# Loading three rows of the fourth tile early, on the second DMA queue, in a layer-norm kernel

## The chip, the cores and the metric

The kernel runs on one core of a Trainium2 chip. The metric is device time in microseconds (us) for one execution. Before the change it is 318.01 us, the median of three runs (317.99 to 318.68).

## The reference

The input `x` is 32 x 512 rows of 1024 floats, 64 MiB (67.11 MB) in all, and every row is normalized by its own mean and variance:

```
mean = np.mean(x, axis=-1, keepdims=True)
var = np.var(x, axis=-1, keepdims=True)
return ((x - mean) / np.sqrt(var + eps)).astype(np.float32)
```

There is no scale and no shift, so nothing but `x` is read, and 67.11 MB are written.

## The kernel before, in words

The 16384 rows are 128 blocks of 128 rows. The kernel calls one block's share of a partition a row, so that a "row" below is 128 partitions x 1024 floats, 512 KiB. Line 11 cuts the 128 rows into 15 tiles of 2 to 10 rows:

```
TILES = (4, 6, 10, 10, 10, 10, 10, 10, 10, 10, 10, 10, 10, 6, 2)
```

In memory, partition p holds K consecutive rows of a tile (`"(p k) d -> p k d"`), so a tile of K rows is, for each partition, one contiguous piece of K x 4 KiB on both sides.

All tiles live in one ring buffer in on-chip memory with room for 50 rows (`RING`). The plan gives each tile its place, starting over at 0 when the tile would not fit. The first six tiles (4 + 6 + 4 x 10 = 50 rows) fill the ring once; the seventh tile lies on the places of the first two, the eighth on those of the third, and so on. Tiles are counted from zero below where they carry a letter: L0 to L14 are the loads and S0 to S14 the stores of tiles 0 to 14. The fourth tile is tile 3.

For each tile, in program order:

- L122: one load of the tile, issued from SyncE (SP), into its place in the ring.
- L68: VectorE (DVE) takes two statistics instructions per row, each over 512 floats.
- L57 to L92: GpSimd (POOL) combines them into minus the mean and the sum of squares, for the whole group of rows at once.
- L95: ScalarE (ACT) takes the square root; L99: DVE the reciprocal; L101: POOL the product of minus the mean and the reciprocal.
- L103: ACT normalizes each row in place, in the ring.
- L127: one store of the tile, issued from ACT's own queue.

A group is a whole tile, except for the last three tiles, where it is at most 6 rows. The order of instructions on each engine is the program's order; it is written out by hand and not planned.

Loads therefore all go through SP's DMA queue (q1 in the profile) and stores all through ACT's (q10). Each load or store counts up one of eight completion semaphores, which the framework gives out in turn. Two kinds of waits come of that. A load into a place that was used before waits until the store of that place has landed: L6 waits for S0 and S1, L7 for S2, L8 for S3. And a transfer that gets a semaphore that an earlier one used waits until that one has landed: in the program before, L5 waits in this way for L0.

Of the kernel before, what the change touches and what calls it, by code (L numbers as in the profile page):

```python
# [1 line left out]

# [4 lines left out]


TILES = (4, 6, 10, 10, 10, 10, 10, 10, 10, 10, 10, 10, 10, 6, 2)  # L10

RING = 50


GROUP = 10
FINE = 6
LAST = 3


@with_exitstack  # L20
def kernel(
    ctx: ExitStack,
    tc: tile.TileContext,
    x: bass.AP,
    eps: bass.AP,
    out: bass.AP,
):
    nc = tc.nc
    P = nc.NUM_PARTITIONS
    eps_val = float(eps) if not isinstance(eps, bass.AP) else 1e-5  # L30

    x2 = x.flatten_outer_dims()
    o2 = out.flatten_outer_dims()
    N, D = x2.shape
    BN_MAX = nc.vector.BN_STATS_FMAX
    NSUB = D // BN_MAX
    H = 2 * NSUB
    assert sum(TILES) * P == N

    rings = ctx.enter_context(tc.tile_pool(name="rings", bufs=1))  # L40
    st = ctx.enter_context(tc.tile_pool(name="st", bufs=3))
    sm = ctx.enter_context(tc.tile_pool(name="sm", bufs=10))

    fdt = mybir.dt.float32
    AF = mybir.ActivationFunctionType
    ALU = mybir.AluOpType

    ring = rings.tile([P, RING, D], fdt)
    eps_t = rings.tile([P, 1], fdt)

    def rows_of(a, row, K):
        return a[row * P : (row + K) * P].rearrange("(p k) d -> p k d", p=P)

    def pool_sum(o, terms):
        G = terms.shape[1]
        half = sm.tile([P, GROUP, 2], fdt, name="half")
        nc.gpsimd.tensor_tensor(  # L57
            out=half[:, :G], in0=terms[:, :, 0:2], in1=terms[:, :, 2:4], op=ALU.add
        )
        nc.gpsimd.tensor_tensor(  # L60
            out=o, in0=half[:, :G, 0], in1=half[:, :G, 1], op=ALU.add
        )

    def group(xs, G):
        stats = st.tile([P, GROUP, NSUB, 6], fdt, name="stats")
        for k in range(G):
            for s in range(NSUB):
                nc.vector.bn_stats(  # L68
                    out=stats[:, k, s, :],
                    in_=xs[:, k, s * BN_MAX : (s + 1) * BN_MAX],  # L70
                )

        parts = stats[:, :G].rearrange("p g s (h c) -> p g (s h) c", h=2)
        mean4, m2 = parts[:, :, :, 1], parts[:, :, :, 2]
        nmean = sm.tile([P, GROUP], fdt, name="nmean")
        dev = sm.tile([P, GROUP, H], fdt, name="dev")
        ss = sm.tile([P, GROUP], fdt, name="ss")
        pool_sum(nmean[:, :G], mean4)
        nc.gpsimd.tensor_scalar(  # L79
            out=nmean[:, :G], in0=nmean[:, :G], scalar1=-1.0 / H, scalar2=None, op0=ALU.mult  # L80
        )
        nc.gpsimd.tensor_tensor(  # L82
            out=dev[:, :G],
            in0=mean4,
            in1=nmean[:, :G].unsqueeze(2).to_broadcast([P, G, H]),
            op=ALU.add,
        )
        nc.gpsimd.tensor_mul(out=dev[:, :G], in0=dev[:, :G], in1=dev[:, :G])  # L88
        nc.gpsimd.tensor_scalar(  # L89
            out=dev[:, :G], in0=dev[:, :G], scalar1=float(D // H), scalar2=None, op0=ALU.mult  # L90
        )
        nc.gpsimd.tensor_tensor(out=dev[:, :G], in0=dev[:, :G], in1=m2, op=ALU.add)  # L92
        pool_sum(ss[:, :G], dev[:, :G])
        std = sm.tile([P, GROUP], fdt, name="std")
        nc.scalar.activation(  # L95
            out=std[:, :G], in_=ss[:, :G], func=AF.Sqrt, bias=eps_t, scale=1.0 / D
        )
        rstd = sm.tile([P, GROUP], fdt, name="rstd")
        nc.vector.reciprocal(out=rstd[:, :G], in_=std[:, :G])  # L99
        nmr = sm.tile([P, GROUP], fdt, name="nmr")  # L100
        nc.gpsimd.tensor_mul(out=nmr[:, :G], in0=nmean[:, :G], in1=rstd[:, :G])  # L101
        for k in range(G):
            nc.scalar.activation(  # L103
                out=xs[:, k, :],
                in_=xs[:, k, :],
                func=AF.Identity,
                bias=nmr[:, k : k + 1],
                scale=rstd[:, k : k + 1],
            )

    plan, row, pos = [], 0, 0
    for K in TILES:
        if pos + K > RING:
            pos = 0
        plan.append((K, row, pos))
        row += K
        pos += K

    with tc.manual_schedule():
        nc.vector.memset(eps_t, eps_val)  # L120
        for t, (K, row, pos) in enumerate(plan):
            nc.sync.dma_start(out=ring[:, pos : pos + K, :], in_=rows_of(x2, row, K))  # L122
            step = FINE if t >= len(TILES) - LAST else GROUP
            for g in range(0, K, step):
                G = min(step, K - g)
                group(ring[:, pos + g : pos + g + G, :], G)
            nc.scalar.dma_start(out=rows_of(o2, row, K), in_=ring[:, pos : pos + K, :])  # L127


# [1 line left out]
_INS = ['x', 'eps']  # L131
_OUTS = [((32, 512, 1024), 'float32')]

_NUMBERS = {'eps': 1e-05}


# [26 lines left out]
```

## Time and profile before

| | |
|---|---|
| median of 3 runs | 318.01 us |
| the profiled execution's own time | 318.5 us |
| its span in the profile | 316.6 us |
| DVE busy | 156.5 us, 49% |
| ACT busy | 152.6 us, 48% |
| POOL busy | 37.5 us, 12% |
| moved by DMA | 134.25 MB, mean 424 GB/s over the span |
| loads, queue q1 | 2160 packets, 67.11 MB, 49.6% of 16 engines' span |
| stores, queue q10 | 2160 packets, 67.11 MB, 49.1% |

The span is the part of the execution that the profile shows, from the first instruction of the program to the last; the other 1.9 us of the profiled execution lie around it. The two queues' shares say how much of the time of the 16 DMA engines went into packets of loads and of stores. Busy shares of DVE, ACT and POOL are for the whole span. A DMA issue shows up twice: as a short instruction on the issuing engine's queue (SPq, ACTq), and as packets on the 16 DMA engines. A load or store has 9 packets on each of these: one for each of the 8 partitions that the engine serves, and one of 4 bytes that counts the semaphore up (2160 = 15 x 16 x 9).

### The profile page before, as it was taken

How to read it: one execution, taken by the hardware profiler on the slowest of the kernel's cores; microseconds unless marked ns; L12 is line 12 of the kernel's file. 1: busy time of each engine (PE TensorE's matmuls, PEld its weight loads, DVE VectorE, ACT ScalarE, POOL GpSimd, SP SyncE). 2: the span in 40 equal slices, each digit the busy share in tenths (PEclk: the TensorE clock that was granted, in tenths of full speed). 3: DMA queues.
4: the chain of work that ended last, by engine and by line, in shares of the span. 5: the costliest groups of instructions: out<-in, count | busy, mean ns of one | idle time of the engine just before them, and what ended most of it. 6: DMA issues, size and time to landing. Idle time of an engine off the chain costs nothing.

```text
span 316.6 us, 712 instructions
## 1 busy us (share of the span) xinstructions
DVE 156.5 (49%) x273; ACT 152.6 (48%) x145; POOL 37.5 (12%) x164
## 2 busy tenths in 40 slices
DVE  0692939539139229229319309409509509654300
ACT  1065329294490391291292192193094094591730
POOL 0202030200300300300300300300300200222200
DMA  8999999999999999999999999999999999999995
GB/s 308 437 424 401 411 466 430 432 419 440 446 435 414 430 457 430 424 419 466 430 424 419 450 435 436 414 430 445 450 414 424 450 438 408 444 421 426 463 407 247
DMA packets 4324, 134.25 MB, mean 424 GB/s; under 512 B 480, under 2 KB 480, under 8 KB 480
## 3 DMA queue, kind: packets, MB, share of 16 engines
q1 hardware_dynamic: 2160, 67.11, 49.6%
q10 hardware_dynamic: 2160, 67.11, 49.1%
q14 instruction: 4, 0.03, 0.0%
HBM read 67.11 MB, written 67.11 MB: 424 GB/s over the span
## 4 chain that ended last, share of the span: by engine, by line
DMA 42%; DVE 26%; another core or an unknown queue 14%; POOL 6%; ACT 5%; issue 3%; SPq 0%; DVEq 0%; POOLq 0%
DMA ring<-in_x_dram 29%; DVE stats L68 26%; DMA out_dram<-ring 13%; ACT ring L103 4%; POOL half L57 1%; POOL dev L89 1%; ACT std L95 1%; POOL dev L92 1%; POOL dev L82 1%; POOL nmean L79 1%; POOL dev L88 1%; POOL nmean L60 1%; POOL ss L60 1%; DVE rstd L99 0%
## 5 line engine op out<-in xcount | busy, mean ns | idle before, releaser
L68 DVE BATCH_NORM_STATS2 stats<-ring 128x6 f32<-128x512 f32 x256 | 153.4, 677 | 92.5 <-DMA ring<-in_x_dram 92.5
L103 ACT ACTIVATE ring<-ring,nmr,rstd 128x1024 f32<-128x1024 f32 x128 | 146.5, 1226 | 8.9 <-POOL nmr L101 8.9
L95 ACT ACTIVATE std<-ss,eps_t 128x10 f32<-128x10 f32 (+3 forms) x16 | 4.8, 301 | 141.7 <-POOL ss L60 141.7
L57 POOL TENSOR_TENSOR half<-stats 128x20 f32<-128x20 f32 (+3 forms) x16 | 3.7, 233 | 243.2 <-DVE stats L68 243.2
L99 DVE RECIPROCAL rstd<-std 128x10 f32<-128x10 f32 (+3 forms) x16 | 3.3, 204 | 51.7 <-ACT std L95 51.7
L89 POOL TENSOR_SCALAR dev<-dev 128x40 f32<-128x40 f32 (+3 forms) x16 | 4.6, 289 | 1.4
L101 POOL TENSOR_TENSOR nmr<-nmean,rstd 128x10 f32<-128x10 f32 (+3 forms) x16 | 3.3, 205 | 10.4 <-DVE rstd L99 10.4
L92 POOL TENSOR_TENSOR dev<-dev,stats 128x40 f32<-128x40 f32 (+3 forms) x16 | 4.1, 259 | 1.3
L79 POOL TENSOR_SCALAR nmean<-nmean 128x10 f32<-128x10 f32 (+3 forms) x16 | 3.9, 244 | 1.4
L82 POOL TENSOR_TENSOR dev<-stats,nmean 128x40 f32<-128x40 f32 (+3 forms) x16 | 3.9, 245 | 1.3
L88 POOL TENSOR_TENSOR dev<-dev 128x40 f32<-128x40 f32 (+3 forms) x16 | 3.8, 239 | 1.3
L57 POOL TENSOR_TENSOR half<-dev 128x20 f32<-128x20 f32 (+3 forms) x16 | 3.4, 212 | 1.3
L60 POOL TENSOR_TENSOR nmean<-half 128x10 f32<-128x10 f32 (+3 forms) x16 | 3.2, 203 | 1.3
L60 POOL TENSOR_TENSOR ss<-half 128x10 f32<-128x10 f32 (+3 forms) x16 | 3.2, 203 | 1.3
L95 ACT ACT_TABLE_LOAD x1 | 1.3, 1283 | 0.9 <-DVE eps_t L120 0.9
L120 DVE MEMSET eps_t<- 128x1 f32 x1 | 0.1, 59 | 0.8 <-PEq L144 0.8
L144 POOL MEMSET const-float32-0.0<- 128x1 f32 x1 | 0.1, 98 | 0.2 <-issue 0.2
L144 POOL MEMSET const-uint8-127<- 128x1 uint8 x1 | 0.1, 102 | 0.0
L144 POOL MEMSET const-bfloat16-1.0<- 128x1 bf16 x1 | 0.1, 101 | 0.0
L144 POOL MEMSET const-float32-1.0<- 128x1 f32 x1 | 0.1, 98 | 0.0
## 6 DMA issues: line engine op xcount, KB each, us to landing
ring<-in_x_dram SPq DMA_DIRECT2D x11, 5120.0 KB, 52.4
out_dram<-ring ACTq DMA_DIRECT2D x11, 5120.0 KB, 41.0
ring<-in_x_dram SPq DMA_DIRECT2D x2, 3072.0 KB, 30.7
out_dram<-ring ACTq DMA_DIRECT2D x2, 3072.0 KB, 22.0
ring<-in_x_dram SPq DMA_DIRECT2D x1, 2048.0 KB, 7.8
out_dram<-ring ACTq DMA_DIRECT2D x1, 2048.0 KB, 22.4
ring<-in_x_dram SPq DMA_DIRECT2D x1, 1024.0 KB, 61.0
out_dram<-ring ACTq DMA_DIRECT2D x1, 1024.0 KB, 11.4
```

Of the source, the lines that this page charges most:

```text
L57: nc.gpsimd.tensor_tensor(out=half[:, :G], in0=terms[:, :, 0:2], in1=terms[:, :, 2:4], op=ALU.add)
L60: nc.gpsimd.tensor_tensor(out=o, in0=half[:, :G, 0], in1=half[:, :G, 1], op=ALU.add)
L68: nc.vector.bn_stats(out=stats[:, k, s, :], in_=xs[:, k, s * BN_MAX : (s + 1) * BN_MAX],)
L79: nc.gpsimd.tensor_scalar(out=nmean[:, :G], in0=nmean[:, :G], scalar1=-1.0 / H, scalar2=None, op0=ALU.mult)
L82: nc.gpsimd.tensor_tensor(out=dev[:, :G], in0=mean4, in1=nmean[:, :G].unsqueeze(2).to_broadcast([P, G, H]), op=ALU.add,)
L88: nc.gpsimd.tensor_mul(out=dev[:, :G], in0=dev[:, :G], in1=dev[:, :G])
L89: nc.gpsimd.tensor_scalar(out=dev[:, :G], in0=dev[:, :G], scalar1=float(D // H), scalar2=None, op0=ALU.mult)
L92: nc.gpsimd.tensor_tensor(out=dev[:, :G], in0=dev[:, :G], in1=m2, op=ALU.add)
L95: nc.scalar.activation(out=std[:, :G], in_=ss[:, :G], func=AF.Sqrt, bias=eps_t, scale=1.0 / D)
L99: nc.vector.reciprocal(out=rstd[:, :G], in_=std[:, :G])
L101: nc.gpsimd.tensor_mul(out=nmr[:, :G], in0=nmean[:, :G], in1=rstd[:, :G])
L103: nc.scalar.activation(out=xs[:, k, :], in_=xs[:, k, :], func=AF.Identity, bias=nmr[:, k : k + 1], scale=rstd[:, k : k + 1],)
```

## The change

The first three rows of tile 3 are taken out of its load and are loaded one by one, 512 KiB each, by three DMAs on ACT's queue, which are the first instructions of that queue. L3 on SP then carries the seven rows that are left. The three are called e0, e1 and e2 below.

```
+EARLY, AHEAD = 3, 3
...
+    def load(engine, t, first, n):
+        K, row, pos = plan[t]
+        engine.dma_start(
+            out=ring[:, pos + first : pos + first + n, :],
+            in_=rows_of(x2, row, K)[:, first : first + n, :],
+        )
+
     with tc.manual_schedule():
         nc.vector.memset(eps_t, eps_val)
+        for k in range(AHEAD):
+            load(nc.scalar, EARLY, k, 1)
         for t, (K, row, pos) in enumerate(plan):
-            nc.sync.dma_start(out=ring[:, pos : pos + K, :], in_=rows_of(x2, row, K))
+            ahead = AHEAD if t == EARLY else 0
+            load(nc.sync, t, ahead, K - ahead)
```

For each partition, e0 to e2 are pieces of 4 KiB, and L3 is one of 28 KiB instead of 40 KiB. In the built program the three further DMAs shift the turn of the eight semaphores. These waits differ at the beginning: L4 now waits until L0 has landed, L5 until e2 has landed (before: L0), S1 until e0 and S2 until e1 have. The statistics of tile 3 wait for e0, e1, e2 and L3 in turn. The waits of L6 and of later loads for stores are the same as before; from S3 on the turn makes a store wait for a store at least three tiles back (S4 for S1, S8 for S4) or for a load (S3 for L2, S9 for L10, the latter as before). The order of instructions on DVE and POOL does not change; on ACT the three issues stand ahead of the load of the activation table.

## The prediction

> **What bounds the kernel now.** I read the page first, then stretches of the span, then the waits of SP's queue and the timeline.
>
> ```profile
> span 316.6 us, 712 instructions
> ...
> DVE 156.5 (49%) x273; ACT 152.6 (48%) x145; POOL 37.5 (12%) x164
> ...
> DMA  8999999999999999999999999999999999999995
> ...
> q1 hardware_dynamic: 2160, 67.11, 49.6%
> q10 hardware_dynamic: 2160, 67.11, 49.1%
> ```
>
> No compute engine reaches half the span, while the two queues together take 98.7% of 16 DMA engines' time. Only the first and last slice are not full, so DMA is the bound from end to end.
>
> ```profile
> core 0: us, DVE busy (x) ACT busy (x) POOL busy (x), PEclk, DMA share, GB/s
> 0.00:4.00 4.00, 0.06 (x1) 1.28 (x1) 0.19 (x4) 1.00 0.61 168
> 4.00:12.00 8.00, 3.44 (x6) 0.00 (x0) 0.00 (x0) 1.00 1.00 430
> 24.00:28.00 4.00, 0.19 (x1) 0.95 (x2) 2.02 (x10) 1.00 0.87 297
> 28.00:60.00 32.00, 24.15 (x41) 17.98 (x17) 2.68 (x11) 1.00 1.02 440
> 100.00:150.00 50.00, 26.04 (x46) 23.45 (x22) 4.86 (x20) 1.00 1.00 433
> 304.00:312.00 8.00, 0.00 (x0) 0.17 (x1) 0.00 (x0) 1.00 0.97 416
> 312.00:316.60 4.60, 0.00 (x0) 0.00 (x0) 0.00 (x0) 1.00 0.32 134
> ```
>
> Each line ends with the DMA share and rate. Loads alone (4 to 12) and both directions together (100 to 150) run at the same 430 to 433 GB/s: the mix doesn't matter. Three places fall short: the start, the end, and 24 to 28, just after the first store is issued (21.58 below).
>
> The trace's packet records say how much. A packet of 40,960 B (ten rows of a partition) takes 1.514 us on its engine, 24,576 B 0.912, 16,384 B 0.611, 8,192 B 0.309, whichever way it goes. A direction has 8 packets per tile and engine: 11 x 8 x 1.514 + 2 x 8 x 0.912 + 8 x 0.611 + 8 x 0.309 = 155.2 us, both 310.4. The first packet starts at 1.75; without a loss the engines would end at 312.2. The last store's 16 landings come at 313.4 to 314.6, the slowest at 315.58, and the span closes 1.0 us later. So the whole loss is 1 to 3 us per engine. Two parts of it are visible. The first packets of q1 take 14.2 engine-us more than their size asks for, 0.9 us per engine. Load packets under way between 22 and 27, while q10 starts its first packets (25.3), take up to 2.28 instead of 1.51, 13.2 engine-us in sum, 0.8 us per engine. Nothing like this comes again while q10 has work: once, when that queue wakes, every engine stands for 0.8 us.
>
> ```profile
> SPq L122 <- DMA out_dram<-ring: 222.2, 9, 35.1
> SPq L122 <- DMA ring<-in_x_dram: 5.2, 1, 5.2
> ```
>
> ```profile
> 21.58 0.37 ACTq L127 DMA_DIRECT2D out_dram<-ring  x1
> 64.16 0.33 SPq L122 DMA_DIRECT2D ring<-in_x_dram  x1
> 299.01 0.34 ACTq L127 DMA_DIRECT2D out_dram<-ring  x1
> 304.19 0.34 ACTq L127 DMA_DIRECT2D out_dram<-ring  x1
> ```
>
> SP waits 222 us for stores, and it costs nothing: L6 is issued at 64.16, when S1 has landed, but L5 keeps q1 busy until 92.4 (by its landings). S13 is issued at 299.01, while S12 runs to 305.9; S14 at 304.19, while S13 runs to 313.2. q10 never empties either, with 7 and 9 us to spare.
>
> **What the Trainium skill says.** All from "DMA: Bandwidth & Descriptors". "Where 436 GB/s comes from": a ceiling of 435 GB/s; 16 x 40,960 B / 1.514 us is 433, so the kernel runs on it. "Issuing engines are not separate DMA queues": transfers from SP and ACT share the same 16 engines and interleave, a second issuer saves only issue time; by this the change moves bytes in time and adds no rate, as the even 430 to 433 of one and of two queues agrees. "Queues, rings and completion order": an engine takes the rows with work in turn, packet by packet. The trace agrees: from 28 to 44, with load packets of 40 KiB against S0's of 16 KiB, 11.1 engines work on loads and 5.0 on stores, near 40 to 16. "Why small descriptors are slow (HBM only)": a fixed cost per packet; the four sizes lie on a line of 37.7 ns per KiB plus 8 ns.
>
> **The change part by part.**
>
> *Bytes and packets.* The bytes stay. Per engine, eight packets of 1.514 (12.11 us) become 24 of 4 KiB and eight of 28 KiB. Neither size is in the trace; the line gives estimates of 0.158 and 1.063, so 3.80 + 8.50 = 12.30: +0.19. Three more DMAs bring each engine three more completion packets, of 9 ns by the records: +0.03. Sum +0.2 us, on the path since engines are always busy. Bounds: 0 (a packet hidden under the other queue's) to +1.6 (60 ns more for each of 24).
>
> *Issue.* Three issues of 0.34 to 0.37 us on ACT delay the table load from 0.93 to about 2.0; it takes 1.28, and ACT's first work is at 16.1. Hidden by 13 us. SP's issues keep their number.
>
> *Order of landing.* Engines turn to data at 1.75 + 0.9 = 2.65, and take packets in turn. L0 with e0: 8 x (0.611 + 0.158) = 6.15, to 8.8, landed at 9.8 (before 8.5). L1 with e1: 8.56, to 17.4, landed 18.3 (15.8). L2 with e2: 8 x 1.672 = 13.4, to 30.8, landed 31.9 (30.0). S0 is issued 13.0 after L0's landing as before, at 22.8 instead of 21.6, but now stands behind e2 in q10: q10 is never empty between e2 and S0. L3 (seven rows) with S0: 8 x (1.063 + 0.611) = 13.4, to 44.2; L3 has landed at 45.5 (47.6). L4 with S1: 8 x 2.426 = 19.4, to 63.6. L5 with S2: 24.2, to 87.8 (L5 landed 92.4 before).
>
> *Cover.* S1 follows L1's landing (+2.5): about 36.5, due 44.2. S2 follows L2 (+1.9): 59.2, due 63.6; this 4.4 us is the least. If it were late, q1 alone would fill the engines, at no cost. Tile 3's statistics wait for four landings, all by 45.5, when DVE is with tile 2 until 47. L4's wait for L0 ends at 9.8, L5's for e2 at 31.9; behind them on SP is L6, which needs S1 (about 64.6). q1 holds L3 and L4 until 63.6 and L5 until 87.8, so these waits have 31 and 23 us of cover; without it each us late would cost at most one. Both queues stay full; in the tail loads end some 3 us earlier and stores run alone longer, at the same rate. The end margins of 7 and 9 us grow.
>
> *Waking q10.* This is the open term. q10 now wakes at about 1.75, together with q1, when engines wait for first packets anyway. If the 0.8 us are the price of waking a queue, they fall into the 0.9 that is lost already: -0.8. If they belong to the first store, S0 pays them at 31: 0. If two wakings come one after the other, the 0.8 only moves to the start: 0 also; a gain at the start, because small packets fill gaps there, is bounded by the 0.9. Thus -1.7 to 0; I take -0.8, since load packets, not stores, show the loss, and a queue's first packets show a like one at 1.75.
>
> *Sum.* +0.2 - 0.8 = -0.6 us. The profiled execution becomes 318.5 - 0.6 = 317.9. The median before is 318.01, 0.5 under the profiled one, so the median after is 317.4.
>
> **Rivals.**
>
> *The stall stays, or moves to the start.* Only +0.2 is left: 318.2. For it: S0 is also the first write of the program. Against: the loss is the same size as that of q1's first packets, which are reads.
>
> *The start gains too.* Half or more of the 0.9, besides the 0.8: 316.6 to 317.1; I set 316.8. For it: first packets of q1 are spread from 1.75 to 3.5, and e0 could fill that. Against: e0's own first packets have to come as well.
>
> *Small packets cost more (the other side).* Place: the first 31 us, where each turn of an engine brings a 4 KiB packet. At 60 ns more than the line: 24 x 0.06 + 0.2 = +1.6, 319.6 with the stall in place, 318.9 without. It decides from 31 ns per packet on, (0.95 - 0.2) / 24, with the stall in place. For it: no packet under 8 KiB of data is in the trace. Against: four sizes lie on one line, and changing queues every packet costs nothing from 60 to 250.
>
> *The change doesn't reach q10 in time,* or a new semaphore wait makes a hole: 318 to 319. Against it is the cover above.
>
> **How the numbers follow.** What this kernel's measurement can tell from no change is 0.3%, 0.95 us: 317.06 to 318.96 is the same. Stall gone 0.42, stall stays 0.26, start gains too 0.16, small packets 0.14, a hole 0.02. Faster: the third, and 0.04 of the first where a little else is gained, 0.20. Slower: small packets and the hole, and 0.02 of the second, 0.18. Same: 0.62. The range of 8 in 10 runs from 316.7, which leaves out the deep part of the third (0.06), to 319.0, which leaves out most of the fourth (0.12). The likeliest case alone is 317.1 to 317.8.
>
> **What would show it.** Right: in 24 to 32 the DMA share is 1.0 and no load packet is stretched; S0 lands near 45, L5 near 89, L0 near 9.8; the last store lands about 0.6 earlier; DMA shares in the middle are unchanged. Wrong: stretched packets when S0 starts (about 31), 4 KiB packets well over 0.16 us, a later first packet than 1.75, or a DMA share below 0.97 anywhere between 4 and 312. The last engine's 1 us lag behind the other fifteen, which I can't explain, would move the time by itself.

## The result, and the profile after

The changed kernel takes 349.19 us (median of four, 349.17 to 349.51) against 318.25 beside it: a ratio of 1.097, with a 95% interval of 1.095 to 1.099. The forecast was 317.4, with 319.0 as its upper end. The loss is 30.9 us.

The page of the changed kernel first, the lines that answer to those shown of before:

```profile
span 347.6 us, 716 instructions
...
DVE 156.6 (45%) x273; ACT 152.6 (44%) x145; POOL 37.5 (11%) x164
...
DMA  7999999999999999999999999999999999948691
...
q10 hardware_dynamic: 2592, 68.68, 50.8%
q1 hardware_dynamic: 2160, 65.54, 44.0%
```

DVE, ACT and POOL are busy for as long as before. DMA looks full until near the end. But two shares changed: stores, with 1.57 MB of early loads beside them, take 50.8% of a longer span, 176.6 us per engine, where they took 155.4; loads take 152.9, where they took 157.0.

Stretches of the changed kernel, with the columns as before (the last two are DMA share and GB/s):

```profile
core 0: us, DVE busy (x) ACT busy (x) POOL busy (x), PEclk, DMA share, GB/s
0.00:4.00 4.00, 0.06 (x1) 1.28 (x1) 0.19 (x4) 1.00 0.52 154
4.00:12.00 8.00, 2.25 (x4) 0.00 (x0) 0.00 (x0) 1.00 1.01 423
28.00:32.00 4.00, 0.33 (x2) 2.99 (x4) 0.56 (x3) 1.00 0.89 322
32.00:60.00 28.00, 23.90 (x41) 15.93 (x15) 2.96 (x13) 1.00 1.01 437
100.00:150.00 50.00, 18.21 (x33) 23.44 (x22) 4.86 (x20) 1.00 0.99 394
280.00:304.00 24.00, 12.14 (x21) 12.93 (x13) 2.51 (x12) 1.00 1.01 429
304.00:312.00 8.00, 1.66 (x4) 6.97 (x7) 1.86 (x9) 1.00 0.34 143
325.00:340.00 15.00, 2.64 (x5) 5.94 (x6) 2.06 (x10) 1.00 0.70 298
```

Between 100 and 150 the share is 0.99 and the rate 394 GB/s; before it was 1.00 and 433. The engines are as occupied as ever and move 9% less: a packet that takes longer counts as busy for longer. From 304 to 312 there is a hole that was not there before.

The packet records show which packets take longer. A record gives start, length, size and queue of a packet, but not its engine; a packet was put to the engine whose last packet ended just as it starts (they overlap by 3 to 4 ns). Below is what one engine does, in order, in each kernel. L is a load packet and S a store packet of 40,960 B with its ns, l and s are the completion packets of a load and of a store (9 ns each); l and s show where the eight packets of a tile end.

```
before, from 105.5 us:   L1514  S1514  L1514  s  L1514  S1514  L1514  S1514  l  S1514  L1514
after,  from 165.0 us:   L1514  S1801  l  s  L1514  S1764  L1514  S1767  L1514
```

In the kernel before, s comes two load packets and two store packets ahead of l: the load and the store that share an engine are three turns out of step. In the changed kernel l and s follow one another: load packet j of one tile and store packet j of another stand back to back, load first. Load packets take 1.514 us in both. Store packets of S2 to S9, the eight that run beside a ten-row load, take 1.76 us in the median instead of 1.514.

The start went as worked out, until then. The timeline, with S2, L6, and the last two stores:

```profile
59.14 0.34 ACTq L140 DMA_DIRECT2D out_dram<-ring  x1
65.68 0.33 SPq L124 DMA_DIRECT2D ring<-in_x_dram  x1
328.30 0.34 ACTq L140 DMA_DIRECT2D out_dram<-ring  x1
333.39 0.34 ACTq L140 DMA_DIRECT2D out_dram<-ring  x1
```

SP's waits in the changed kernel:

```profile
SPq L124 <- DMA out_dram<-ring: 225.1, 8, 33.2
SPq L124 <- DMA ring<-in_x_dram: 29.1, 2, 22.0
```

The two new waits, L4 for L0 and L5 for e2, are there with 29.1 us in sum, and they delay nothing. The wait for stores is as long as before.

How 0.25 us per packet becomes 31 us: eight store packets per tile make 2.0 us more on an engine, and on fourteen engines a tile takes 26.1 us (loads of tiles 6 to 12 complete at 116.14 to 272.79 in the median, six tiles) instead of 24.2.

Two engines do worse. Their store packets take 2.00 us, and their landings of S3 to S9 come 28.1 us apart, 3.9 more than before. They fall behind: by 2.9 us at L6 and 17 at L14, whose last landing is at 324.96 against 307.68 on the other fourteen. A load has landed when its last engine is done. So the other engines run out of work from 304 on, while tile 13 and then tile 14 wait for these two, and the statistics of the last tile start 29.2 us later than before (the kernel before first, then the changed one):

```profile
295.89 2.47 DVE L68 BATCH_NORM_STATS2 stats<-ring 128x6 f32<-128x512 f32 x4 [4.12 <-DMA ring<-in_x_dram]
325.08 2.48 DVE L71 BATCH_NORM_STATS2 stats<-ring 128x6 f32<-128x512 f32 x4 [4.02 <-DMA ring<-in_x_dram]
```

The sum on these two engines: 30 us from L5 to L12, and 2.8 more at L13, where S10 runs beside it. There seven of S10's eight packets, 40,960 B each, take 1.80 to 2.14 us behind load packets of 24,576 B; on the other fourteen engines the same packets take 1.514. Against that, the loads were 2.9 us ahead at L4 (median landing 64.58, before 67.47). About 30 are left, and they are the 29.2 at the last tile. The remaining 1.9 of the span come after it, as the two engines also finish S12 and S13 late.

### The profile page after: what moved, and what is told of

It reads as the page before. It is cut to its first block, busy times and chain, and to the rows that moved or that the text cites. A ratio compares the mean times of both kernels' runs of the same rounds, so it can differ in the third digit from the quotient of the medians.

```text
span 347.6 us, 716 instructions
## 1 busy us (share of the span) xinstructions
DVE 156.6 (45%) x273; ACT 152.6 (44%) x145; POOL 37.5 (11%) x164
## 3 DMA queue, kind: packets, MB, share of 16 engines
q10 hardware_dynamic: 2592, 68.68, 50.8%
## 4 chain that ended last, share of the span: by engine, by line
another core or an unknown queue 41%; DMA 36%; DVE 10%; ACT 4%; POOL 3%; issue 1%; SPq 1%; POOLq 0%; DVEq 0%
DMA ring<-in_x_dram 23%; DMA out_dram<-ring 13%; DVE stats L71 10%; ACT ring L106 4%; SPq L124 1%; POOL half L60 1%; POOL dev L92 0%; POOL dev L95 0%; POOL nmean L82 0%; POOL dev L85 0%; POOL dev L91 0%; ACT std L98 0%; POOL nmean L63 0%; POOL ss L63 0%
```

## The experiments

Theory A is that the turns are what costs: store packet j right behind load packet j on an engine. Theory B is that the early rows do it, by their small packets or by the early use of ACT's queue. A leaves open which memory the two packets collide in: that of the inputs and outputs (A1), or on-chip memory, where packet j of any full load or store would belong to the same partition of its engine (A2). That is taken from the two being cut over the engines in the same way; the packet records name no partition.

### Two early rows, twice

```
-EARLY, AHEAD = 3, 3
+EARLY, AHEAD = 3, 2
```

> The changed kernel with two rows loaded early instead of three. In the profile of the changed kernel store packets of 40,960 B take about 1.76 us from 68 us on, against 1.51 before, and at every tile the completion packets of a load and of a store now fall together (90.11 and 90.12), where before the store was 6.0 us, two turns of the engines, ahead. Theory A, the turns: what costs is that on each engine load packet j and store packet j of two ten-row tiles follow one another; three early rows bring it about, because e2 holds S0 back until L3 begins. With two early rows S0 starts inside L2, two or three packets off, and the time is 318 to 319. Theory B, the early rows: small packets or the early use of ACT's queue slow the stores; then two rows keep most of the loss, 338 to 349. If the time is 349 with the completions apart, A falls.

Measured: 318.01, 346.53, 346.24 and 347.15 us. The same program has both times. The profiled execution is the one of 318.01; its store packets take 1.514, and s leads l by two turns (`L1514 s L1514 S1514 l S1514`). None of the three long ones has a profile. One more execution, with a profile:

> The kernel with two early rows once more, for a profile: its four times before were 318.01, 346.53, 346.24 and 347.15, and only the first has a profile, with completions of stores 3.0 us ahead of loads and store packets at 1.51 us. Theory A: a profile of about 346 has the completions together, load first, and store packets at 1.7 us and more; one of 318 has them apart. If a profile of 346 has them apart, A falls.

Measured: 334.4, a third time. In the median over engines s still leads l, by 3.0 us. But on one engine of the sixteen the completions are together, and its store packets take 1.79 us in the median. That the executions of 346 us are the same with more such engines is likely, but not shown. Landings of four DMAs, median of all engines and last engine:

```
        median   last engine
L7      138.8    143.48
S4      135.7    143.66
L11     235.5    249.75
S8      232.4    249.94
```

That engine falls behind, by 14.3 us at L11, and everything ends up waiting for it. Stretches of this run:

```profile
100.00:200.00 100.00, 45.00 (x79) 46.88 (x44) 9.72 (x40) 1.00 1.00 431
280.00:292.00 12.00, 8.32 (x15) 5.27 (x6) 2.62 (x12) 1.00 0.90 390
292.00:300.00 8.00, 4.63 (x9) 6.86 (x7) 1.75 (x9) 1.00 0.08 33
300.00:312.00 12.00, 4.85 (x10) 5.91 (x6) 2.23 (x10) 1.00 1.02 437
```

The rate is full for almost all of the run, with nothing to be seen in it. But L12 lands at 276.06 on the one engine, when most others have had it since 260, so the statistics of tile 12 start at 276.18 and its store is issued at 299.64. By 292 the other engines have nothing left to do, and DMA stands almost still for 8 us (33 GB/s). One engine in step, of sixteen, goes with a loss of 16 us. This also speaks against a limit that the engines share: the others write at their usual pace beside the slow one. What decides, from one execution to the next, in which turn S0 enters was not found; with two early rows S0 enters in the middle of L2.

### One turn off, on either side, with all three early rows

First S0 as two stores of 64 partitions:

```
+            cuts = (0, P // 2, P) if t == 0 else (0, P)
+            for lo, hi in zip(cuts, cuts[1:]):
+                nc.scalar.dma_start(
+                    out=rows_of(o2, row, K)[lo:hi], in_=ring[lo:hi, pos : pos + K, :]
+                )
```

> The changed kernel with S0 cut into two stores of 64 partitions each, so that it has 10 packets per engine instead of 9; all three early rows stay. Theory A: every later store is one packet behind the load it goes with (load packet j beside store packet j - 1), completions 3 us apart, load first; the slow store packets are gone and the time is 318 to 320. Theory B: nothing that B blames is changed, 347 to 350. In between (325 to 345): one packet off is not far enough, and the price depends on the distance.

Measured: 320.16 us, ratio 1.007 (1.0045 to 1.0095). An engine's packets read `L1514 S1514 l S1514 L1514 s L1514 S1514`: store packet j - 1 behind load packet j, all at 1.514. Of the loss of 31 us 2 are left, whose cause was not looked for, with every early row in place.

Then the seven rows of L3 as two loads of 64 partitions:

```
+            cuts = (0, P // 2, P) if t == EARLY else (0, P)
+            for lo, hi in zip(cuts, cuts[1:]):
+                nc.sync.dma_start(
+                    out=ring[lo:hi, pos + ahead : pos + K, :],
+                    in_=rows_of(x2, row, K)[lo:hi, ahead:K, :],
+                )
```

> The changed kernel with the seven rows of L3 loaded by two DMAs of 64 partitions each: 10 packets per engine instead of 9 on SP's queue. Theory A: every later store is one packet ahead of its load (load packet j beside store packet j + 1), completions 3 us apart, store first; 318 to 320. Theory B: 347 to 350. Together with the cut of S0 it shows whether the sign of the distance matters.

Measured: 324.79 us, ratio 1.021 (1.019 to 1.023). The packets read `L1514 s l S1514 L1514 S1514`: the completions are together, and still no ten-row packet is slow. The store stands first here, so that store packet j + 1 follows load packet j. Being close isn't enough; the order counts. Its profile shows where the 6 us over the others are:

```profile
28.00:40.00 12.00, 7.54 (x14) 7.20 (x7) 0.49 (x3) 1.00 0.96 289
40.00:52.00 12.00, 8.39 (x15) 3.81 (x5) 2.44 (x10) 1.00 1.03 313
100.00:200.00 100.00, 51.61 (x90) 46.90 (x44) 9.77 (x40) 1.00 1.00 433
```

While the halves of L3 are under way the rate is 289 to 313 GB/s, and 433 afterwards. The load packets of the halves take 1.72 us in the median instead of 1.06, and S0's packets beside them 0.78 instead of 0.61. So the cost comes with cutting this load into lower and upper partitions. The same cut of S0, in the run before, left its packets at 0.611.

### Other sources in the input

```
+    def moved(t):
+        return plan[t][0] if 5 <= t <= 12 else 0
...
+            in_=x2[row * P + moved(t) : (row + K) * P + moved(t)].rearrange(
```

> The changed kernel, but tiles 5 to 12 are read from addresses in x that lie ten rows of 4 KiB (40,960 B) further on, so that each partition gets the next one's rows; what is computed for these tiles is the normalization of other rows. Places in on-chip memory, packet sizes and turns stay, the completions still fall together. Theory A1: load and store packets in step collide in the memory of the inputs and outputs, because their addresses there differ by the same amount at every packet; moved sources change that amount and the time comes down, to 318 to 325. Theory A2: they collide in on-chip memory, where both touch the same partition at once; nothing of that changes, 347 to 350.

Measured: 349.58 us, ratio 1.099, with tiles 5 to 12 computed from other rows. Store packets take 1.76 to 1.78 as in the changed kernel. A1 has no support left from the side of the sources; destinations in the output were not moved.

### The turns alone, without an early row

```
+            if t == 0:
+                nc.scalar.dma_start(out=spare[0:32, :], in_=x2[0:32, 0:128])
             nc.scalar.dma_start(out=rows_of(o2, row, K), in_=ring[:, pos : pos + K, :])
```

> The kernel before, without any early row, with one small load (32 partitions x 512 B, to a place that nobody reads) on ACT's queue just ahead of S0: three more packets per engine, so that every store comes three turns later against its load. In the kernel before, the completion of a store leads that of the load beside it by four packets (109.45 and 115.48), which is three turns from the changed kernel's order, where store packet j follows load packet j. Theory A, the turns: that order is restored without a single early row, store packets take 1.7 us and more, and the time is 340 to 350. Theory B, the early rows and small packets: 16 KiB more cost nothing, 318 to 319. If some engines land one turn beside the order, a time between 319 and 349.

Measured: 318.07 us, ratio 0.999. It tests nothing. The small load was through at 24.16 and S0 at 41.78, in the median of the engines, S0 as before: ACT's queue was empty, and the three packets were gone before S0's first one. The turns did not move (l and s 6.0 us apart as before). The same load one store later, `if t == 1:`, stands behind S0 in a queue that is not empty:

> The kernel before, without any early row, with the small load of 32 partitions (three packets per engine) ahead of S1 instead of ahead of S0. Ahead of S0 it had landed (24.16) before S0's first packet and moved nothing: completions of stores still led by 6.0 us. Ahead of S1, ACT's queue is still busy with S0, so S1 and all later stores come three turns later. In the kernel before, the packets of one engine read L, S, L, s (completion of the store), L, S, L, S, l; three turns later store packet j follows load packet j. Theory A: completions together, load first, store packets at 1.7 us and more, 335 to 350. Theory B (early rows): 318 to 319. If completions are together and the time is 318, A falls.

Measured: 349.37 us, ratio 1.098 (1.097 to 1.100). That is the loss of the changed kernel, from 16 KiB of unread data in the kernel before. The packets read `L1514 S1787 l s L1514 S1796 L1514`, and the stretches are those of the changed kernel:

```profile
40.00:64.00 24.00, 14.26 (x26) 14.37 (x15) 4.89 (x20) 1.00 1.00 433
100.00:150.00 50.00, 18.07 (x33) 23.44 (x22) 4.89 (x20) 1.00 1.00 400
304.00:312.00 8.00, 1.30 (x3) 6.83 (x7) 1.75 (x8) 1.00 0.48 202
```

One engine of the sixteen is an exception, and a test of its own: on it the stores come one turn later (store packet j - 1 behind load packet j), its packets take 1.514 us, and its loads land 24.3 us apart, while the others need 26.2 and two of them 28.1. Theory B is gone. The reverse, all of the change but out of step, was run in two forms:

```
         for k in range(AHEAD):
             load(nc.scalar, EARLY, k, 1)
+        nc.scalar.dma_start(out=spare[0:16, :], in_=x2[0:16, 0:128])
```

> The changed kernel with one small load (16 partitions x 512 B, unread) on ACT's queue behind e2: two more packets per engine ahead of S0, so that store packet j - 2 follows load packet j. All that the change does is still done. Theory A: 317.5 to 319, store packets at 1.51 us. Theory B: 347 to 350.

Measured: 317.98 us, ratio 0.9993 (0.9985 to 1.0001), packets `S1514 l S1514 L1514 S1514 L1514 s`. With 112 partitions instead of 16:

> As the run with two packets, but with eight (112 partitions x 512 B): one turn short of a whole store, so store packet j + 1 follows load packet j. The run with L3 in halves had that order, but with a slow spell of its own between 31 and 51 us. Theory A: 318 to 320. If one turn off on this side is slow as well: 330 to 350. Theory B: 347 to 350.

Measured: 317.95 us, ratio 0.9990 (0.9983 to 0.9996). The turns were not those that I had meant. L3 went with the small load, L4 with S0 and L5 with S1, each pair completing together (39.61, 56.73 and 76.09), and then SP's queue ran dry, since L6 has to wait for S1. L6 came late, and the rest is four turns out of step on most engines (`s L1514 S1514 L1514 S1514 L1514 S1514 l`). From 76 to 80 loads occupied 0.6 engines and stores 15.4: a dry queue beside a full one costs nothing. This is the only run whose interval lies below the kernel before, by 0.1%.

### Same turns, other partitions

Loads and stores in two halves, even partitions and then odd ones:

```
+            for h in ((0, 1) if t > EARLY else ()):
+                nc.sync.dma_start(
+                    out=ring[h:P:2, pos : pos + K, :], in_=rows_of(x2, row, K)[h:P:2]
+                )
...
+            for h in ((0, 1) if t > 0 else ()):
+                nc.scalar.dma_start(
+                    out=rows_of(o2, row, K)[h:P:2], in_=ring[h:P:2, pos : pos + K, :]
+                )
```

> The changed kernel with every load from L4 and every store from S1 cut in two by partitions, even ones first, then odd ones, in the same order for loads and stores. An engine still takes load packet j and store packet j after one another, and both still touch the same partition. Theory A2 (a store packet reads the partition of on-chip memory that the load packet just ahead of it writes): slow, 335 to 360. If it is 318 to 322 although the completions fall together, the cut itself takes the loss away, and the next run tells nothing.

Measured: 345.44 us, ratio 1.086 (1.084 to 1.087); `L1514 S1789 l s L1514 S1772 L1514`. The cut leaves the loss in place. From about 210 us on loads run alone for a while, the turns shift, and packets are back at 1.514; a part of this run's loss is the hole that follows (DMA share 0.63 from 280 to 304). Then with `(1, 0)` in place of `(0, 1)` in the stores:

> As the run before, but with odd partitions first in the stores, even ones first in the loads: the same packets in the same turns, with load packet j and store packet j in different partitions. Theory A2: store packets at 1.51 us, 318 to 324. A theory in which the turns alone count, or the sizes, or that an engine's reads and writes alternate in this order: as slow as the run before.

Measured: 321.90 us, ratio 1.012 (1.010 to 1.014); `L1514 S1514 l s L1515 S1539`: the same turns, load first, completions together (173.20 and 173.21), and no slow packet from 60 to 240 us. The rate in the same stretch, for the same order and then for the opposite one:

```profile
100.00:150.00 50.00, 18.02 (x32) 23.44 (x22) 4.89 (x20) 1.00 1.00 395
```

```profile
100.00:150.00 50.00, 26.03 (x46) 23.44 (x22) 4.89 (x20) 1.00 1.00 433
```

So the turns alone do not cost anything. It takes a store packet that reads the partition to which the load packet just ahead of it has written. This is A2, with the partitions inferred as said above: exchanging the halves of the stores alone takes the price away, as A2 says it must. 23.5 us lie between the two runs. The opposite order also changes by one partition which input addresses go with which output addresses; the moved sources had changed that too, without effect.

### Other places in the same partitions

```
+    GAP = {20: 256, 30: 256, 40: 512}
+    def place(pos, first, n):
+        at = (pos + first) * D + GAP.get(pos, 0)
```

> The changed kernel, but the places of the ten-row tiles in the ring are moved apart: 1 KiB further for those at rows 20 and 30, 2 KiB for those at row 40, so that the distance in a partition between a load's place and the place of the store beside it is no longer a whole number of rows, for every pair from L5 and S2 on. (The pool of small tiles has 6 buffers instead of 10 to make room.) Turns, sizes and partitions stay. If the same partition is what counts, wherever in it the two lie: 347 to 350. If the collision needs a distance of whole rows of 4 KiB: 318 to 325, as with opposite halves, or in between where only some pairs are freed.

Measured: 361.84 us, ratio 1.137. The store packets of S2 to S9 take 1.753 to 1.768 us in the median, as in the changed kernel (1.754 to 1.764): where in the partition the two lie makes no difference. The further 12.7 us are a fault of the edit. The gap moved tile 13 by 1 KiB into tile 14's place, so that L14 had to wait for S13, and its median completion is at 346.0 instead of 307.0.

## Why the prediction was wrong

**What bounds the kernel** was right: DMA from end to end. The reading of it was not. The step that failed is "the mix doesn't matter", together with "whichever way it goes". I had one set of turns in front of me, three out of step, and took its 1.514 us for a property of the packet. It was a property of the order: directly behind the load packet of the same partition the same store packet takes 1.76 us, and 2.00 on two engines.

**The order of landing** was right almost to the digit, and held the clue. L0 was to land at 9.8, L1 at 18.3, L2 at 31.9, L3 at 45.5; they landed at 9.7, 18.4, 31.8 and 45.4. S1 was issued at 36.23 (36.5 worked out; the terms given, 34.28 + 2.5, make 36.8) and S2 at 59.14 (59.2). The same lines said that L3 with S0 end together at 44.2, L4 with S1 at 63.6, L5 with S2 at 87.8. So the change was seen to put both queues in step, by holding S0 behind e2 until L3 began. From that I took that both queues stay full. I did not ask what being in step might do, which nothing in the trace of before shows. L5 was to land near 89 and landed at 91.9: the first pair of ten-row packets is where the two part.

**Bytes, packets and issue** were right: a 4 KiB packet takes 0.159 us (estimate 0.158), one of 28 KiB 1.062 (1.063). The rival with dear small packets had no ground.

**Cover** was right for every wait. The two new ones cost nothing, and the run whose SP queue went dry lost nothing.

**Waking the queue** was wrong, by a small sum. I put the 0.8 us on q10's first use. In the changed kernel q10 is in use from 2.9 us on, and packets that run while S0 starts still take 9.6 engine-us too long, 0.6 per engine, where it was 13.8 (packets between 20 and 60). So it does not all come with the queue's first use. It need not come with the first store either: in the run with eight packets, where q10 carried small packets until S0, the sum from 20 to 60 is only 4.0 engine-us. The cause stays open. The start took 12.6 engine-us against 14.3. The saving is 0.4 us per engine, not 0.8, and at +0.2 for packets it leaves what the run with two packets suggests, 0.9993, with an interval that still holds 1.

**What would show it wrong** named a DMA share below 0.97. The share does fall below that, to 0.89 from 28 to 32 while S0 starts, and to 0.34 in the hole from 304 to 312. Between 100 and 250, where the time is lost, it is 0.99 to 1.01 while up to 9% of the rate is gone. The rate, or the time of a packet, was the sign to name.

**The rivals** missed it: a chance of 0.18 for slower, all of it on prices of 1 or 2 us. That a transfer's price may depend on which transfer of the other queue stands before it was not among them.

What is shown and what isn't. Shown: the order makes the loss without the change, and the change makes no loss without the order; the order costs only if the two packets are of the same partition, as far as the partitions can be inferred; places inside it don't matter; one engine alone is enough. Open: what happens inside the engine or the memory, why two engines pay 0.49 us instead of 0.25, and why S1 behind L4 (24,576 behind 40,960 B, in step, same partitions) and S0 behind L3 pay nothing (912 and 611 ns). On fourteen engines only pairs of equal size, 40,960 B, were seen to pay; on the other two S10 behind L13 (40,960 behind 24,576 B) paid as well.

## What to carry to other kernels

When two DMA queues are both full, as here, a change at the start of one can set in which turn they meet for the rest of the program. In this kernel one small DMA moved the time by 10%, or back. Where loads and stores have the same shape, look at the order of the completions of the load and the store that run side by side: here a load completion directly ahead of the store's was the sign, and one more packet on either queue cured it. Judge a DMA-bound stretch by GB/s and by the time of a packet, not by the share of busy engines.

## What the runs showed of the hardware

- A 40,960 B store packet right behind an equally large load packet of the same partition took 1.76 us on fourteen engines and 2.00 on two, against 1.514 in any other order seen (store packet j - 1, j - 2, or j + 1 to j + 4 behind load packet j). The Trainium skill ("DMA: Bandwidth & Descriptors", "The descriptor swizzle") puts the eight partitions of an engine on one port. By that, the other packets of an engine use the same port, and behind them the store packet took 1.514: sharing the port is not enough to make it slow. No record here shows the port.
- The Trainium skill ("Perfetto Trace Analysis", "What "DMA-bound" means") lists reading from on-chip memory as a possible but unlikely bound. Here a store's packets, which read from it, lost 14% of their pace for that order alone, while load packets lost nothing. Whether it is the reading that they waited for is not shown.
- A DMA is done when its slowest engine is. One engine 14.3 us behind at L11 left the rate at 431 GB/s for as long as the others had work, and then it fell to 33 GB/s for 8 us.
- Two loads of 64 neighbouring partitions each (28,672 B packets) ran at 289 to 313 GB/s, all queues together, beside a store of 128. Loads and stores cut into even and odd partitions kept 433 (40,960 B packets, opposite order).
